# Three unused pads that shift the start addresses of the wide products' operands in SBUF

## The chip, the core and the metric

The kernel runs on one core of a Trainium2 chip. The core has five engines that run beside each other and meet through semaphores: TensorE (PE in the profile, its weight loads shown apart as PEld), VectorE (DVE), ScalarE (ACT), GpSimd (POOL) and SyncE (SP, which here issues nearly all DMAs). Operands lie in SBUF, 128 partitions wide; a tile takes the same byte range in each partition, so its place is one start address. Products go to PSUM.

The metric is the device time of one execution in microseconds, the median of several runs. Before the change it is 1610.83 us over three runs, from 1602.51 to 1612.37.

## The reference

One layer of an encoder block on 1024 tokens of width 1024, in float32:

```python
h = rms_norm(h_res, norm_w[layer])
z = jnp.einsum('bsd,dc->bsc', h, w_in[layer])
qkv_a, g_a, q_b, zf_fwd, zf_bwd, i_b, g_b, zgate_a, zgate_b = jnp.split(z, split_points, axis=-1)
...
y_a = jnp.einsum('bsc,cd->bsd', o_a * jax.nn.silu(g_a), w_proj_a[layer])
...
y_b = jnp.einsum('bsc,cd->bsd', o_b, w_proj_b[layer])
merged = jax.nn.sigmoid(zgate_a) * y_a + jax.nn.sigmoid(zgate_b) * y_b
h_res = h_res + jnp.einsum('bsd,de->bse', merged, w_out[layer])
```

Three groups of windowed attention (dilations 1, 4 and 16) give o_a; a gated linear recurrence in both directions gives o_b. Most of the arithmetic is the four dense products: the input projection (1024 by 12288), the two branch projections and the output projection.

## The kernel before

**Wide products.** Each dense product is cut into matmuls with a stationary operand of 128x128 and a moving operand of 128x512. To keep float32 accuracy every operand is split into a rounded part and the rest (float32r tiles: whi and wlo for the weights, hhi and hlo for the normalised input, sh and sl or mh and ml for later inputs), and three matmuls are run for each block: high with high, high with low, low with high. There are 5496 such matmuls. ScalarE rounds, GpSimd or VectorE subtracts, and a page of 128x512 weights is then used by 24 matmuls.

Which operand moves depends on the stage. In `tok_group` (line 773) the weights move and slices of hhi and hlo, 128 tokens each, are stationary; for the second and third attention group `tok_view` (line 760) takes tokens with a stride of 4 or 8 elements. In `T_group` (line 785) hhi and hlo move and the weights are stationary. `run_quads` (line 425) computes most of the two branches' merging gates by block products with sums of halves (tiles S0 to S3, each with a high and a low part). At the end `three` (line 1704) runs the branch projections, with sh and sl moving, and the last loop runs the output projection, with the weights moving and mh and ml stationary. Only the first four value tiles, at the very start, use uhi and ulo.

**Order.** All instructions pass through one helper (`call`, line 54 and 55, so that the profile shows every instruction at L55), which keeps a plan of each engine's time. A scheduler in Python (`Builder`) fills the gaps between wide products with small ones (scores, transposes, the recurrence) when the plan says that their inputs are ready. The plan is worked out from sizes and types; it does not look at addresses. The result is a fixed order on each engine, with semaphores where one engine needs another.

**Stages**, in us of the profiled execution: opening and first attention group to about 200, second group to about 390, third to about 600, gates and early pages with the merging of the attention groups to 829, block products 829 to 943, recurrence with its projections about 970 to 1370, branch projections to 1513, output projection to the end.

**Where the tiles lie.** SBUF is handed out from two stacks, in the order in which pools and tiles are declared, each tile rounded up to 32 bytes. The left stack begins at 16512, behind a reserved range and four constants:

```python
    consts = ctx.enter_context(tc.tile_pool(name="consts", bufs=1))
    wpool = ctx.enter_context(tc.tile_pool(name="wts", bufs=1))
    stg = ctx.enter_context(tc.tile_pool(name="stg", bufs=3))
    tiny = ctx.enter_context(tc.tile_pool(name="tiny", bufs=2))
```

consts holds nw, hwc, ident and nqk: 32 + 32 + 512 + 32 = 608 bytes. wts (raw, whi, wlo) and stg hold tiles of 2048 bytes. tiny is 2624 bytes long. Behind it come the pools of each stage, one after another at the same place. The right stack begins at 229344 and grows downwards; hhi and hlo, 32768 bytes each, are its first tiles, and the S sums or the tail's sh and sl stand below or in place of them. This gives the start addresses of before, modulo 128 bytes:

| tiles | region | start modulo 128 |
|---|---|---|
| ident | left, consts | 64 |
| raw, whi, wlo, stage | left, wts and stg | 96 |
| hhi, hlo, S0 to S3 | right | 96 |
| sh, sl of the second branch | right | 96 |
| sh, sl of the first branch, mh, ml, uhi, ulo | left, behind tiny | 32 |
| ig, qr, km, sk, kT of the attention, s, pT, zn, v | left, behind tiny | 32 |
| S, xa, on, kT of the recurrence | left, behind tiny | 96 |
| dg (moving operand of rB, `spread`, line 691) | left, behind tiny | 0 |

Of the kernel before, what the change touches and what calls it, by code (L numbers as in the profile page):

```python
# [8 lines left out]
F32 = mybir.dt.float32  # L9
# [555 lines left out]
def hybrid_block(ctx, tc, a, out):  # L565
    b = Builder(ctx, tc, a)
    a_, v_, g_, t_, s_ = b.p.act, b.p.dve, b.p.pool, b.p.pe, b.p.sp
# [4 lines that stand above are left out]
# [2 lines left out]
    bps = ctx.enter_context(tc.tile_pool(name="bps", bufs=5, space=PSUM))  # L574
    b.gps = b.ring(gps, "g", 3, [128, 512])
    b.bank = b.ring(bps, "b", 5, [128, 512])
    hctx = ExitStack()
    hpool = hctx.enter_context(tc.tile_pool(name="hT", bufs=1, side="right"))
    ctx.enter_context(tc.manual_schedule())
# [1294 lines left out]
def _build(arrays):  # L1874
    import concourse.bacc as _bacc
    nc = _bacc.Bacc("TRN2", target_bir_lowering=False, num_devices=1)
    args = {n: nc.dram_tensor(f"in_{n}_dram", v.shape, mybir.dt.from_np(v.dtype), kind="ExternalInput").ap()
            for n, v in arrays.items()}
    out = nc.dram_tensor("out_0_dram", (S, D), F32, kind="ExternalOutput").ap()
    with tile.TileContext(nc) as tc:  # L1880
        hybrid_block(tc, args, out)
    return nc
# [9 lines left out]
```

## Time and profile before

| | before |
|---|---|
| median of three runs | 1610.83 us |
| lowest and highest | 1602.51 and 1612.37 us |
| profiled execution | 1608.46 us |
| its span, first to last instruction | 1606.6 us |
| mean granted TensorE clock | 0.99 |
| LDWEIGHTS and MATMUL instructions | 8373 each |
| moved by DMA | 148 MB in 110,879 packets |

A row of the timeline gives the start in us, the length, the engine, the operation with out<-in (the moving operand is named first, the stationary one second), the shapes and how many alike were merged; in brackets stand idle time before it and what ended that. A row of a group gives busy time and the mean of one in ns, then the idle time before. Starts of matmuls are recorded, their ends are modelled, so the length of one (389 ns) is more than the distance to the next start.

### The profile page before, as it was taken

How to read it: one execution, taken by the hardware profiler on the slowest of the kernel's cores; microseconds unless marked ns; L12 is line 12 of the kernel's file. 1: busy time of each engine (PE TensorE's matmuls, PEld its weight loads, DVE VectorE, ACT ScalarE, POOL GpSimd, SP SyncE). 2: the span in 40 equal slices, each digit the busy share in tenths (PEclk: the TensorE clock that was granted, in tenths of full speed). 3: DMA queues.
4: the chain of work that ended last, by engine and by line, in shares of the span. 5: the costliest groups of instructions: out<-in, count | busy, mean ns of one | idle time of the engine just before them, and what ended most of it. 6: DMA issues, size and time to landing. Idle time of an engine off the chain costs nothing. (4 is left out here: it accounts for less than half of the span.)

```text
span 1606.6 us, 23188 instructions
## 1 busy us (share of the span) xinstructions
PE 1569.1 (98%) x8373; PEld 1335.8 (83%) x8373; DVE 845.3 (53%) x2216; ACT 659.5 (41%) x1434; POOL 468.0 (29%) x462
## 2 busy tenths in 40 slices
PE   8899999999999999999899999999999999999999
PEld 6688899999999987678788888888877878888887
DVE  5667632575136642336412207988889887543211
ACT  5533542434334363213334437655565554422110
POOL 3411202202022031228434434433344423003320
PEclk9999999999999999899999999999999999999999
DMA  6402203102022035473413251121221211842232
GB/s 215 139 22 98 70 18 112 50 33 67 21 63 66 16 103 138 125 219 112 144 66 115 83 166 40 53 93 40 54 86 47 94 39 65 293 140 92 88 119 89
DMA packets 110879, 148.31 MB, mean 92 GB/s; under 512 B 24625, under 2 KB 48300, under 8 KB 110764
## 3 DMA queue, kind: packets, MB, share of 16 engines
q1 hardware_dynamic: 103340, 146.38, 29.1%
q8 instruction: 66, 1.08, 0.3%
q10 hardware_dynamic: 7424, 0.45, 0.3%
q14 instruction: 49, 0.40, 0.1%
HBM read 110.77 MB, written 40.73 MB: 94 GB/s over the span
## 5 line engine op out<-in xcount | busy, mean ns | idle before, releaser
L55 POOL TENSOR_TENSOR wlo<-raw,whi 128x512 fp32r<-128x512 f32 x192 | 253.9, 1328 | 685.8 <-ACT whi L55 670.4
L55 PE MATMUL gp<-whi,hhi 128*128 128x512 f32 x792 | 328.5, 415 | 8.3 <-ACT stage L55 5.7
L55 PE MATMUL gp<-wlo,hhi 128*128 128x512 f32 x792 | 316.0, 399 | 1.4 <-POOL wlo L55 1.4
L55 PE MATMUL gp<-whi,hlo 128*128 128x512 f32 x792 | 316.1, 399 | 0.0
L55 PEld LDWEIGHTS gp<-whi,hhi 128*128 128x128 f32 x792 | 200.5, 253 | 36.8 <-issue 10.0
L55 PEld LDWEIGHTS gp<-wlo,hhi 128*128 128x128 f32 x792 | 201.4, 254 | 18.3 <-POOL wlo L55 2.6
L55 PEld LDWEIGHTS gp<-whi,hlo 128*128 128x128 f32 x792 | 200.9, 254 | 17.9 <-DVE hlo L55 1.0
L55 PE MATMUL gp<-hhi,whi 128*128 128x512 f32 x512 | 209.4, 409 | 0.0
L55 PE MATMUL gp<-hhi,wlo 128*128 128x512 f32 x512 | 200.9, 392 | 0.0
L55 PE MATMUL gp<-hlo,whi 128*128 128x512 f32 x512 | 200.0, 391 | 0.0
L55 ACT ACTIVATE whi<-raw 128x512 fp32r<-128x512 f32 x192 | 119.3, 626 | 140.9 <-PE gp L55 81.7
L55 PEld LDWEIGHTS gp<-hhi,wlo 128*128 128x128 f32 x512 | 96.2, 188 | 21.3
L55 PEld LDWEIGHTS gp<-hhi,whi 128*128 128x128 f32 x512 | 96.8, 189 | 18.8 <-issue 1.0
L55 PEld LDWEIGHTS gp<-hlo,whi 128*128 128x128 f32 x512 | 96.8, 189 | 17.2
L55 ACT ACTIVATE s<-s,neg 128x192 f32<-128x192 f32 (+2 forms) x192 | 83.9, 439 | 65.5 <-DVE neg L55 65.3
L55 DVE TENSOR_REDUCE ss<-sq 128x8 f32<-128x512 f32 x48 | 32.8, 684 | 146.7 <-ACT sq L55 146.7
L55 POOL TENSOR_TENSOR wlo<-qraw,whi 128x512 fp32r<-128x512 f32 x42 | 55.0, 1316 | 76.9 <-ACT whi L55 76.7
L55 PE MATMUL gp<-sh,whi 128*128 128x512 f32 x192 | 75.0, 391 | 0.0
L55 PE MATMUL gp<-sh,wlo 128*128 128x512 f32 x192 | 74.9, 390 | 0.0
L55 PE MATMUL gp<-sl,whi 128*128 128x512 f32 x192 | 74.6, 389 | 0.0
L55 ACT ACTIVATE sq<-gp 128x512 f32<-128x512 f32 x48 | 28.0, 592 | 111.8 <-PE gp L55 91.4
L55 ACT ACTIVATE stage<-gp 128x512 f32<-128x512 f32 x48 | 28.0, 594 | 111.5 <-PE gp L55 88.3
(225 smaller groups left out, 2787.9 us busy)
## 6 DMA issues: line engine op xcount, KB each, us to landing
raw<-in_w_in_dram SPq DMA_DIRECT2D x168, 256.0 KB
igD<-stage SPq DMA_DIRECT2D x32, 256.0 KB
ig<-igD SPq DMA_DIRECT2D x32, 256.0 KB
sgl<-sgD SPq DMA_DIRECT2D x32, 256.0 KB
oD<-os SPq DMA_DIRECT2D x48, 128.0 KB
og<-oD SPq DMA_DIRECT2D x24, 256.0 KB
qraw<-in_w_in_dram SPq DMA_DIRECT2D x24, 256.0 KB
sgD<-spare SPq DMA_DIRECT2D x24, 256.0 KB
```

Source lines behind the costliest of these rows:

```text
L55: got = f(*args, **kw)
```

## The change

Three tiles are declared that no instruction writes or reads.

```diff
     b.gps = b.ring(gps, "g", 3, [128, 512])
     b.bank = b.ring(bps, "b", 5, [128, 512])
+    top = ctx.enter_context(tc.tile_pool(name="top", bufs=1, side="right"))
+    top.tile([128, 24], F32, name="topPad")
+    consts.tile([128, 8], F32, name="lowPad")
+    tiny.tile([128, 16], F32, name="tinyPad", bufs=1)
     hctx = ExitStack()
     hpool = hctx.enter_context(tc.tile_pool(name="hT", bufs=1, side="right"))
```

lowPad takes 32 bytes at the start of consts, so ident, the weights, stage and tiny begin 32 bytes later. tinyPad takes 64 bytes at the start of tiny, so everything behind tiny begins 96 bytes later. topPad takes 96 bytes at the top of the right stack, so everything on that side begins 96 bytes lower. Modulo 128 the wide products' tiles then begin at 0 in all regions, ident at 96, ig, qr, km and sk at 0, S, xa and on at 64, and dg at 96.

## The prediction

> **What bounds the kernel now.** I read the page's busy shares and its 40 slices first, then the timeline of TensorE (matmuls and weight loads), the groups by form, the sums by windows, and last the waits.
>
> ```profile
> span 1606.6 us, 23188 instructions
> PE 1569.1 (98%) x8373; PEld 1335.8 (83%) x8373; DVE 845.3 (53%) x2216; ACT 659.5 (41%) x1434; POOL 468.0 (29%) x462
> PE   8899999999999999999899999999999999999999
> PEclk9999999999999999899999999999999999999999
> ```
>
> TensorE is busy in 98% of the span at a granted clock of nearly 1, so the time is the number of its instructions times the distance from one start to the next. 5496 of its 8373 matmuls are wide products, a moving operand of 128x512 float32r. Busy time can't give that distance (the ends are modelled and overlap); the timeline's starts can. Here is the block-product stage, where every operand of both kinds starts at 96 modulo 128 bytes:
>
> ```profile
> 829.21 0.39 PE L55 MATMUL qA<-hhi,whi 128*128 128x512 f32 x1
> ...
> 834.65 0.39 PE L55 MATMUL qA<-S1h,whi 128*128 128x512 f32 x1
> ```
>
> There are 24 products from the first start to the last: 5.44 / 24 = 226.7 ns each. Under the half clock, early in the kernel, the distance is another (first a stretch of the windows view: length, PE busy, granted clock, DMA; then the timeline):
>
> ```profile
> 30.00:36.00 6.00, 5.44 (x17) 0.50 0.47 171
> ```
> ```profile
> 32.86 0.63 PE L55 MATMUL u<-wlo,uhi 128*128 128x512 f32 x1
> 33.29 0.63 PE L55 MATMUL u<-whi,ulo 128*128 128x512 f32 x1
> 33.71 0.63 PE L55 MATMUL u<-whi,uhi 128*128 128x512 f32 x1
> ```
>
> 0.85 / 2 = 425 ns for 512 columns, 0.83 ns a column. At the full clock 512 columns would need half of that, 213 ns, and take 226.7. So some 13 ns are not columns through the array: they are hidden when the array runs slowly and show when it runs fast. That is what a feed of the moving operand that can't quite keep up looks like. Is it the next weight load, read at the same time?
>
> ```profile
> 767.68 0.39 PE L55 MATMUL gp<-whi,hlo 128*128 128x512 f32 x1
> 773.75 0.80 PE L55 MATMUL gp<-whi,hhi 128*128 128x512 f32 x1 [5.68 <-ACT stage L55]
> ```
> ```profile
> 767.46 0.19 PEld L55 LDWEIGHTS gp<-whi,hlo 128*128 128x128 f32 x1
> 773.75 0.29 PEld L55 LDWEIGHTS gp<-whi,hhi 128*128 128x128 f32 x1 [6.10 <-ACT stage L55]
> ```
>
> No weight load runs beside the product at 767.68, the next comes 6 us later, and it still lasts 0.39 us like those in the chain. So the 13 ns belong to the moving stream itself. 226.7 / 213.3 is 17 / 16, and 2048 bytes that begin 32 bytes short of a 128-byte boundary touch 17 such pieces instead of 16. That arithmetic carries the forecast; it is an inference, no row here shows an aligned wide product.
>
> Do start addresses matter at all? Two stages of before have other starts. With the stationary operand (mh, ml) at 32 and the moving one at 96, and then with the moving operand (sh, sl) at 32 and the stationary one at 96:
>
> ```profile
> 1520.09 0.40 PE L55 MATMUL gp<-whi,mh 128*128 128x512 f32 x1
> ...
> 1523.59 0.39 PE L55 MATMUL gp<-whi,mh 128*128 128x512 f32 x1
> ```
> ```profile
> 1390.29 0.39 PE L55 MATMUL gp<-sh,whi 128*128 128x512 f32 x1
> ...
> 1392.35 0.39 PE L55 MATMUL gp<-sh,whi 128*128 128x512 f32 x1
> ```
>
> 3.50 / 15 = 233.3 ns and 2.06 / 9 = 228.9 ns, against 226.7, for the same shapes and types. So the starts do count, by 2 to 7 ns.
>
> Two attention groups have stationary operands with a stride (4 or 8 elements between columns):
>
> ```profile
> 219.64 0.39 PE L55 MATMUL gp<-whi,hhi 128*128 128x512 f32 x1
> ...
> 222.22 0.40 PE L55 MATMUL gp<-whi,hlo 128*128 128x512 f32 x1
> ```
> ```profile
> 408.94 0.41 PE L55 MATMUL gp<-whi,hhi 128*128 128x512 f32 x1
> ...
> 411.63 0.41 PE L55 MATMUL gp<-whi,hlo 128*128 128x512 f32 x1
> ```
> ```profile
> L55 PEld LDWEIGHTS qA<-hlo,whi 128*128 128x128 f32 x47 | 8.8, 188 | 1.8
> L55 PEld LDWEIGHTS gp<-whi,hhi 128*128 128x128 f32 x157 | 48.7, 310 | 1.9 <-issue 1.9
> L55 PEld LDWEIGHTS gp<-whi,hhi 128*128 128x128 f32 x176 | 57.9, 329 | 2.2 <-issue 1.4
> ```
>
> 2.58 / 11 = 234.5 ns (stride 4) and 2.69 / 11 = 244.5 ns (stride 8). Their loads last 310 and 329 ns against 188, longer than the distance: there the weights are likely the limit, not the stream.
>
> **The change part by part.** It adds three tiles that nobody writes or reads: no instruction, DMA, wait or semaphore. The order on every engine is worked out from sizes and not from addresses, so it stays. What moves are start addresses: everything in the left stack behind lowPad by 32 bytes, behind tinyPad by 96, everything in the right stack by 96 downwards. whi, wlo, hhi, hlo, the S sums, uhi, ulo, mh, ml, sh and sl all come to 0 modulo 128 (the strided views start 4r bytes further).
>
> The target distance. The only wide moving operand at 0 modulo 128 in this trace is dg, in two passes at two cycles a column:
>
> ```profile
> 53.31 1.02 PE L55 MATMUL rB<-dg,ones 128*128 128x512 f32 x2
> L55 PE MATMUL rB<-dg,ones x4: 591/592/593, 38.5 to 53.7; 128*128 128x512 f32 x4
> ```
>
> (The second row is from the view of the tile rB.) Start to start is 1.02 - 0.59 = 0.43 us for 1024 cycles, 427 by the array: an excess of some 2 to 3 ns. It streams at half the rate, so it doesn't prove the point, but it is the nearest row. I take 215.7 ns; the bounds are 213.3 (all excess gone) and 233.3 (0 modulo 128 as bad as the mh pairing).
>
> [...]
>
> The terms, products counted from the loops:
> - Both at 96, contiguous: 3648 products, 11.0 ns each: 40.1 us.
> - Moving 96, stationary 32: 504, of which 96 lie in the opening 48 us, whose pace loads and preparation set (taken as nothing); 408 x 17.6 = 7.2 us.
> - Moving 32, stationary 96: 192 x 13.2 = 2.5 us.
> - Strided: 2 x 576. Bounds 0 (weights limit) and 11 ns (stream limits); the loads' row is nearer, so I take 3 ns: 3.5 us, bounds 0 and 12.7.
> - Other operands move too. ident goes from 64 to 96; if a stream of 512 bytes pays a quarter of 13.4 ns, 691 transposes cost 2.3 us; those that read ig, S, qr and pT (now at 0 or 64) could win as much. Taken as nothing, bounds -2.3 and 2.3. DVE, ACT and POOL work on the same shapes; none of them bounds.
>
> Sum: 53.3 us off TensorE's own time. What of it reaches the end?
>
> ```profile
> 48.00:200.00 152.00, 149.12 (x850) 119.09 (x849) 99.10 (x358) 67.81 (x184) 34.05 (x31) 1.00 0.27 84
> 970.00:1100.00 130.00, 126.78 (x780) 106.17 (x779) 112.93 (x234) 79.44 (x148) 55.21 (x69) 0.99 0.19 58
> 1200.00:1300.00 100.00, 96.12 (x641) 81.74 (x641) 86.62 (x192) 55.19 (x101) 37.33 (x47) 1.00 0.20 64
> PE gp L55 <- ACT stage L55: 5.7, 1, 5.7
> PE U L55 <- ACT kT L55: 5.5, 4, 2.6
> PE oB L55 <- DVE S L55: 5.4, 4, 3.2
> ```
>
> (Columns of the first three: stretch, then busy time of PE, PEld, DVE, ACT, POOL. The last three are waits: total, times, longest.) In the recurrence stage, 970 to 1370, DVE is 87% busy and TensorE already waits for it. A DVE chain behind each head doesn't shorten, so I let a third of that stage's gain (1174 products, 12.9 us) be lost: 4.3. The stage wait that ends at 773.75 stands behind some 690 products since 600 us, which gain 7.6 us; if the stores that free the buffers don't come sooner, the wait grows by that; I take 3. The early attention, where DVE is two thirds busy, 1 us. Lost: 8.3. Bounds of the loss: nothing, and 12.9 + 7.6 if others set both stretches.
>
> 53.3 - 8.3 = 45.0 us. The profiled execution took 1608.46 us (1606.6 of span and 1.9 around it): 1563.5. It lies 2.4 below the median of the runs shown, 1610.83. Forecast: 1563.
>
> **The rivals.**
> (a) The 13 ns don't come from the start. They could be the price of four-byte operands at the full clock, wherever they begin; no row excludes it, since all wide streams of before start at 32 or 96. For it: the starts 96 and 32 both pay about the same 13 ns. Against it: the exact 17 / 16, and that pairings of starts move the distance. Then only the mixed pairings go to 226.7: 408 x 6.6 + 192 x 2.2 = 3.1 us, 1605. [...]
> (b) Slower. A weight load starts one distance ahead of its product (767.46 and 767.68 above), so beside the whole stream before it; with both at 0 modulo 128 the two streams could collide as at 96 with 32. Price: 6.6 ns on each of 3648 products, 24 us, and 192 x 4.4 = 0.8; no gain elsewhere: 1633. Against it: 96 with 96, the same phase, has the lowest distance of all. It decides against me from a distance above 226.7 in the block stage; above 231 (16 / 3648 is 4.4 ns more) it is slower by over 1%.
> (c) The stream gets shorter but is eaten: the strided products gain nothing, and the recurrence and the stretch ahead of the stage wait keep their length, set by DVE, ACT and the stores. For it: the waits shown. Against it: TensorE is 96 to 98% busy there and the others 87% at most. Left: 53.3 - 3.5 - 12.9 - 7.6 = 29.3 us, 1579.
> (d) The pads don't land where meant. The lengths (608 + 32 bytes of consts, 2624 + 64 bytes of tiny, 96 at the top) come to multiples of 128, so I give it nothing.
>
> **How the numbers follow.** The forecast's case gets 0.48, (c) 0.17, (a) 0.27, (b) 0.08. The time is the first's. Its own range is 1536 (213.3 on the 4248 contiguous products: 10.2 us more; strided by 11 ns: 9.2; no losses: 8.3; together 1535.8) to 1575. The range must take in (c) and (a) with its bound of 2.3 for ident: 1536 to 1607. What a measurement of this kernel can tell from no change is about 1%, 16 us. Faster by over 1%: 0.48 + 0.17 = 0.65. Within 1%: (a), 0.27. Slower: (b), 0.08.
>
> **What would show it.** In the changed kernel the block stage decides: 24 products there in 5.18 us is right, 5.44 is rival (a), more than that (b). The mh stage should fall to the same distance as the block stage. Strided distances near 234 and 244 with loads of 310 and 329 ns say that weights bind there; a fall by 11 says that the stream did. Waits of U and oB for DVE and the stage wait should be longer by some 8 us in all. The same instruction count and the same order must be found. The forecast is wrong if the distance at 0 modulo 128 stays at 226.7.

## The result, and the profile after

| | before | after |
|---|---|---|
| median | 1610.40 us | 1622.84 us |
| lowest and highest of six runs | 1602.51 and 1612.37 us | 1621.90 and 1624.14 us |
| span of the profiled execution | 1606.6 us | 1620.3 us |
| mean granted TensorE clock | 0.990 | 0.993 |

The changed kernel takes 1.0084 times as long as the one before (95% interval 1.0063 to 1.0105): about 13 us slower, where 45 us faster were forecast. Instructions (23188) and DMA traffic (110879 packets, 148.31 MB) are the same. From the page of the changed kernel, the span and the busy times:

```profile
span 1620.3 us, 23188 instructions
PE 1586.2 (98%) x8373; PEld 1339.9 (83%) x8373; DVE 845.4 (52%) x2216; ACT 659.7 (41%) x1434; POOL 467.8 (29%) x462
```

Against before, PE has 17 us more and VectorE, ScalarE and GpSimd are within 0.3 us. So the time was added by TensorE's own instructions. The block-product stage was named as the place that decides; its timeline in the changed kernel (start, length, operation), the same two products as were shown of before:

```profile
833.56 0.39 PE L55 MATMUL qA<-hhi,whi 128*128 128x512 f32 x1
...
839.14 0.39 PE L55 MATMUL qA<-S1h,whi 128*128 128x512 f32 x1
```

24 products in 5.58 us: 232.5 ns each, where before had 5.44 and 5.18 was hoped for. Taken from all starts, the distance isn't constant now: it repeats over seven products, 232, 231, 232, 228, 230, 233 and 241 ns, 232.4 in the mean. The same mean stands at every wide chain of the changed kernel, the output projection (whi with mh) included, which before had 233.3:

```profile
1532.00 0.40 PE L55 MATMUL gp<-whi,mh 128*128 128x512 f32 x1
...
1535.48 0.39 PE L55 MATMUL gp<-whi,mh 128*128 128x512 f32 x1
```

3.48 / 15 = 232.0 ns. All stages came to one distance, as the prediction expected of equal starts, but to a worse one. The whole difference, from the distances between all starts of matmuls in the two traces, in us (a chain is a run of wide products that follow each other without a wait or another kind of product between them):

| distances | before | after |
|---|---|---|
| wide, contiguous, inside chains | 4039 of 228.41 ns: 922.6 | 4046 of 232.39 ns: 940.3 |
| the same, 262 ns and longer (waits, half clock, a group's first) | 73.7 | 69.2 |
| the same, to another kind of product | 41.9 | 41.0 |
| strided by 4, inside chains | 536 of 235.1 ns: 126.0 | 536 of 239.2 ns: 128.2 |
| strided by 8, inside chains | 534 of 244.9 ns: 130.8 | 534 of 245.6 ns: 131.2 |
| all else | 306.4 | 305.4 |

The products inside chains cost 17.7 + 2.6 us more (1.6 of it because seven more of them fall into the first row), and 6 to 7 us of that come back in the other rows, which leaves the 13.7 by which the span grew. By stage, with the same product marking the ends in both kernels:

| stage of before, us | wide contiguous products | after minus before, us |
|---|---|---|
| to 48 | 122 | -0.2 |
| 48 to 200 | 454 | +1.3 |
| 200 to 600 (mostly strided) | 96 | +2.7 |
| 600 to 829 | 864 | +0.5 |
| 829 to 970 | 622 | +3.6 |
| 970 to 1370 | 1174 | +3.1 |
| 1370 to 1513 | 628 | +3.1 |
| 1513 to the end | 383 | -0.4 |

Between 829 and 970, where TensorE waits for nothing (no distance above 227 ns before and 241 ns after), the 622 products pay 5.7 ns each, the full step from 226.7 to 232.4. From 600 to 829 almost all of it is given back. The windows of that stretch, before and then after (stretch, length, busy time of PE, PEld, DVE, ACT, POOL, granted clock, DMA share, GB/s), and TensorE's waits after (total, times, longest):

```profile
600.00:829.00 229.00, 219.18 (x957) 174.06 (x954) 88.11 (x112) 64.10 (x119) 82.81 (x59) 0.96 0.45 135
```
```profile
600.00:829.00 229.00, 221.35 (x958) 173.13 (x957) 86.50 (x112) 66.60 (x129) 80.06 (x57) 0.97 0.44 135
```
```profile
PE oB L55 <- DVE S L55: 5.3, 4, 3.2
PE U L55 <- ACT kT L55: 4.6, 3, 2.1
PE gp L55 <- ACT stage L55: 4.5, 1, 4.5
```

TensorE comes to the stage wait 4.3 us later than before (at 772.37 us, before at 768.07), and the wait ends 3.1 us later (776.84, before 773.75): it fell from 5.7 to 4.5 us, and over the whole stretch the distances of 262 ns and more, of products with 512 columns, fell from 36.5 to 31.9 us. Part of that is pace: 17 wide distances of the stretch are at half pace (400 to 450 ns), where before had 23, and the granted clock is a little higher (0.97, before 0.96). That isn't simply because the waits are shorter: behind the shorter stage wait there are 8 of them, where before had 6. The other two rows are waits of the recurrence, which had 5.4 (oB) and 5.5 us (U) before.

### The profile page after: what moved, and what is told of

It reads as the page before. It is cut to its first block, busy times and chain, and to the rows that moved or that the text cites. A ratio compares the mean times of both kernels' runs of the same rounds, so it can differ in the third digit from the quotient of the medians.

```text
span 1620.3 us, 23188 instructions
## 1 busy us (share of the span) xinstructions
PE 1586.2 (98%) x8373; PEld 1339.9 (83%) x8373; DVE 845.4 (52%) x2216; ACT 659.7 (41%) x1434; POOL 467.8 (29%) x462
## 2 busy tenths in 40 slices
DMA packets 110879, 148.31 MB, mean 92 GB/s; under 512 B 24625, under 2 KB 48300, under 8 KB 110764
```

## The experiments

The block stage had become slower at 0 with 0 modulo 128, as rival (b) has it. Whether that is the reason was asked of wide products with nothing else beside them first; the theory that came out of the first table (what counts is how far the start of the weights lies from that of the moving operand, modulo 256) was then tested against (b) and against the forecast's own reason. Four kernels measure wide products alone, five move the tiles of the kernel itself.

**t1_table: all pairings of starts.** The kernel is replaced: only chains of 84 wide products that add up in one PSUM tile, nothing beside them, and the output is the last sum. The moving tile starts at 0, 32, 64 or 96 modulo 128 (A to D), the stationary one likewise.

```diff
+    for m in "ABCD":
+        for w in "ABCD":
+            last = chain("p" + m + w, mov[m], sta[w])
```

> This kernel computes nothing of the reference: it runs 16 chains of 84 wide float32r products (128x512 moving, 128x128 stationary) with nothing beside them, one chain for each pair of start addresses 0, 32, 64, 96 modulo 128 of the moving and the stationary operand, and stores one of the results. Theory 1, the pairing of the two starts sets the distance of wide products by itself: the four pairs known from the two traces come out as there (moving 96 with stationary 96: 226.7 ns; 96 with 32: 233.3; 32 with 96: 228.9; 0 with 0: 232.4), and the other twelve fill the table, some perhaps below 226.7. Theory 2, the extra distance in the changed kernel comes from other traffic whose tiles moved too: all sixteen are alike, within 1 ns. My forecast's 17/16 rule would give 213 to 216 for every pair whose moving operand starts at 0; the 0 with 0 stage of the changed kernel has already contradicted it.

The timeline, some of the chains (start, length of the whole chain, name, and how many products):

```profile
26.39 19.68 PE L39 MATMUL pAA<-mA,wA 128*128 128x512 f32 x84
45.91 19.75 PE L39 MATMUL pAB<-mA,wB 128*128 128x512 f32 x84
65.50 19.39 PE L39 MATMUL pAC<-mA,wC 128*128 128x512 f32 x84
84.72 19.76 PE L39 MATMUL pAD<-mA,wD 128*128 128x512 f32 x84
...
299.94 19.83 PE L39 MATMUL pDC<-mD,wC 128*128 128x512 f32 x84
319.60 19.68 PE L39 MATMUL pDD<-mD,wD 128*128 128x512 f32 x84
```

From start to start a chain AA takes 19.52 us, 232.4 ns a product; AC 19.22, 228.8; DC 19.66, 234.0. Means over the last 42 distances of each chain, in ns:

| moving \ stationary | A | B | C | D |
|---|---|---|---|---|
| A | 232.4 | 233.3 | 228.9 | 233.3 |
| B | 234.3 | 232.4 | 233.3 | 228.9 |
| C | 233.3 | 234.3 | 232.4 | 233.3 |
| D | 233.3 | 233.3 | 234.3 | 232.4 |

All four diagonal fields are equal: 0 with 0 is no worse and no better than 96 with 96. And 96 with 96 gives 232.4 here, though before's block stage, 96 with 96 as well, ran at 226.7. So the start modulo 128 doesn't settle the distance, neither as the forecast had it nor as (b) had it. Modulo 256 the two cases differ: here the moving tiles start at 128, 160, 192 and 224, the stationary ones at 0, 32, 64 and 96, so that on the diagonal stationary minus moving is 128. In before hhi and whi both start at 224 modulo 256, difference 0; in the changed kernel at 128 and 0. Fields of the table with the same difference modulo 256 have nearly the same value: 192 gives 228.9 twice, 96 gives 234.3 three times, 128 gives 232.4 four times. Before's own mixed stages fit in: sh with whi is difference 192 and had 228.9, whi with mh is 64 and had 233.3.

**t2_width: element size and length.** Again chains alone, with bfloat16 operands, and with float32r at 512 columns and fewer.

```diff
+    for m, w in ("AA", "BB", "DD", "DB", "DA", "AD"):
+        chain("b" + m + w, bm[m], bw[w])
+    for n in (512, 448, 384, 256, 128):
+        for m, w in ("AA", "DD", "DB"):
+            chain("n..." + m + w, mov[m], sta[w], n)
```

> This kernel computes nothing of the reference either: chains of 63 products, first bfloat16 operands at 512 columns for six pairs of starts (0/0, 32/32, 96/96, 96/32, 96/0, 0/96), then float32r at 512, 448, 384, 256 and 128 columns for the pairs 0/0, 96/96 and 96/32. If the excess over columns / 2.4 GHz belongs to reading four bytes a column, bfloat16 shows some 216 ns for every pair, and with float32r the excess (13 to 20 ns at 512) shrinks in proportion with the columns (3 to 5 ns at 128). If it is a fixed cost for each product or for each weight load, bfloat16 or the narrow products keep 13 ns or more.

The timeline (four chains of 63), then two groups of weight loads (busy time, mean of one in ns):

```profile
35.45 13.76 PE L47 MATMUL bBB<-bmB,bwB 128*128 128x512 bf16 x63
49.04 13.76 PE L47 MATMUL bDD<-bmD,bwD 128*128 128x512 bf16 x63
...
118.07 14.86 PE L47 MATMUL nhDD<-mD,wD 128*128 128x512 f32 x63
132.76 14.87 PE L47 MATMUL nhDB<-mD,wB 128*128 128x512 f32 x63
```
```profile
L47 PEld LDWEIGHTS <-bwB 128*128 128x128 bf16 x126 | 12.3, 98 | 14.9
L47 PEld LDWEIGHTS nhAA<-mA,wA 128*128 128x128 f32 x63 | 11.9, 188 | 2.8
```

bfloat16: 13.59 / 63 = 215.7 ns, and 215.8 for all six pairings. float32r at the same 512 columns: 14.69 / 63 = 233.2. So the aligned distance that the forecast took for float32r exists, but for bfloat16, and there it needs no alignment. A bfloat16 load lasts 98 ns, a float32r load 188. With fewer float32r columns the two differences 128 and 64 give 203.8 and 202.2 ns (448), 175.9 and 174.7 (384), 118.7 and 113.3 (256), and 111.7 for both at 128. The columns' own time is an estimate from the half clock of before (granted clock 0.50 from 30 to 36 us), where the timeline has

```profile
32.86 0.63 PE L55 MATMUL u<-wlo,uhi 128*128 128x512 f32 x1
...
35.42 0.63 PE L55 MATMUL u<-wlo,uhi 128*128 128x512 f32 x1
```

Six products take 2.56 us, 426.7 ns each; half of that is 213.3 ns for 512 columns, and fewer in proportion. The excess over it is 15 to 20 ns from 384 columns up and 7 to 12 at 256. It neither goes with the length nor is it constant. DD at 512 columns had 233.3 here and 232.4 in t1_table with the same addresses, with another repeating pattern: a chain can settle into more than one.

**t3_diff: the difference in steps of 16 bytes.** One moving tile, and a wide tile of weights from which the stationary start is moved by 16 bytes from chain to chain (ra to rp); then fewer weight columns, and strides.

```diff
+    for k in range(16):
+        chain("r" + letters[k], m, W[:, 4 * k:4 * k + 512])
```

> This kernel computes nothing of the reference: chains of 57 float32r products with the stationary start moved against a fixed moving start in 16 steps of 16 bytes (differences 0 to 240 modulo 256), some of them again after other chains, then chains with only 64 or 32 stationary columns, with a stationary stride of 4 and 8, and single products that each wait for ScalarE, float32r and bfloat16. Theory D, the moving stream and the next weight load hinder each other, and what counts is the difference of their starts modulo 256: 226.7 ns at difference 0, 232.4 at 128, 228.9 at 192, 233.3 at 64 as in the first table; fewer stationary columns bring the distance down toward 216; a single float32r product, with no load beside its stream, is as long as a bfloat16 one (379 ns). Rival I, float32r operands cost 11 ns at the full clock in any case and only the rest is pairing: fewer columns stay at 226 or more, and a single float32r product keeps some 389 ns against 379.

The timeline, chains of 57 (ra, rb, rc, rd: differences 0, 16, 32, 48; ri: 128; halfa, halfi: 64 weight columns, differences 0 and 128):

```profile
24.32 13.08 PE L47 MATMUL ra<-mA,W 128*128 128x512 f32 x57
37.24 13.09 PE L47 MATMUL rb<-mA,W 128*128 128x512 f32 x57
50.17 13.45 PE L47 MATMUL rc<-mA,W 128*128 128x512 f32 x57
63.47 13.45 PE L47 MATMUL rd<-mA,W 128*128 128x512 f32 x57
...
129.93 13.47 PE L47 MATMUL ri<-mA,W 128*128 128x512 f32 x57
143.23 13.46 PE L47 MATMUL rj<-mA,W 128*128 128x512 f32 x57
...
314.32 13.27 PE L62 MATMUL halfa<-mA,W 128*64 128x512 f32 x57
327.42 13.34 PE L62 MATMUL halfi<-mA,W 128*64 128x512 f32 x57
```

ra: 12.92 / 57 = 226.7 ns. rb: 12.93, 226.8. rc: 13.30, 233.3. ri: 13.30, 233.3 (232.4 in two repeats). Of the other differences 176 gives 230.1, 240 gives 228.3, 192 gives 233.3 and in two repeats 228.9, and the rest 232.1 to 234.3. So the moving tile at 128 modulo 256 has the fast distance as soon as the weights start there too. Nothing goes below 226.7. Shorter loads don't free the rest: at difference 0, 64 weight columns (loads of 134 ns) have 13.10 / 57 = 229.8, and 32 columns (109 ns) have 231.7 over their last 42 distances, both more than the 226.7 of full loads of 188 ns. Of the expectation's two signs, that of rival I came (226 or more), and theory D's fall toward 216 did not. Strided weights have 235.0 (stride 4) and 244.4 ns (stride 8) alone as in the kernel. Single float32r products that each wait 0.72 us for ScalarE lasted 0.40 to 0.49 us in the first four and 0.80 us from the sixth on, bfloat16 ones 0.58 us after a first of 0.65. With such a spread they can't be held against the 389 and 379 ns of the expectation.

**t4_next: what a product takes over from the one before, and finer steps.** Groups of one float32r product and three of bfloat16; chains whose weights alternate between differences 0 and 128 one by one (swap) or in pairs (pairs); differences of 8, 4, 12 and 252 bytes (fine, finer, finest, back).

```diff
+    for name, offs in (("swap", (0, 32)), ("pairs", (0, 0, 32, 32)), ("fine", (2,)), ("finer", (1,)), ("finest", (3,)), ("back", (63,))):
+        for q in range(REP):
+            s = offs[q % len(offs)] + 128 * (q % 4)
+            nc.tensor.matmul(p, W[:, s:s + 128], m, start=(q == 0), stop=(q == REP - 1))
```

> This kernel computes nothing of the reference. First, one float32r product (difference 0, then 128) followed by three bfloat16 products, over and over: the load beside the float32r stream is a bfloat16 one. If the 13 ns at difference 0 and the 19 at 128 come from the float32r load beside the stream, the distance from a float32r product to the next start falls to about 216 ns in both; if the stream pays its 13 ns alone, it stays at 226.7 in both and only the 6 above it go; if neither is so, 232 stays at difference 128. Then chains whose stationary start alternates between differences 0 and 128 (each load against the same moving operand): a mean near 229 to 233 ns if each product pays for its own pair. Then differences of 4, 8, 12 and 252 bytes: 226.7 if what counts is a 16-byte piece or coarser, as the 0 and 16 of the 16-byte table were alike.

The timeline, chains of 57:

```profile
114.94 13.31 PE L64 MATMUL fine<-mA,W 128*128 128x512 f32 x57
128.09 13.41 PE L64 MATMUL finer<-mA,W 128*128 128x512 f32 x57
141.34 13.28 PE L64 MATMUL finest<-mA,W 128*128 128x512 f32 x57
154.46 13.46 PE L64 MATMUL back<-mA,W 128*128 128x512 f32 x57
167.75 13.09 PE L46 MATMUL end<-mA,W 128*128 128x512 f32 x57
```

fine 230.7, finer 232.5, finest 230.2, back 233.2 ns, by the starts; by their last 42 distances swap has 232.2, pairs 232.9, end (difference 0) 226.7. A difference of 16 bytes was as good as none (226.8 in t3_diff), one of 4, 8 or 12 wasn't. Alternating doesn't give the mean of both distances (229.5 to 230) but the slow one. It lies in the 229 to 233 that were expected, but it speaks against each product paying for its own pair alone: what stands before or behind it in the chain has a part. The mixed groups are inconclusive: a group of four takes 0.90 us with difference 0 and with 128; three bfloat16 distances and one of 226.7 would be 0.87, so the groups take 0.03 us more than that, which is more than the 6 ns that were looked for.

**e_top128: before with 128 bytes at the top of the right stack.** No start of a wide operand changes modulo 128, but hhi, hlo and the S sums now differ from the weights by 128 modulo 256.

```diff
+    top = ctx.enter_context(tc.tile_pool(name="top", bufs=1, side="right"))
+    top.tile([128, 32], F32, name="topPad")
```

> Before with one pad of 128 bytes at the top of the right stack: every start modulo 128 is as before, but hhi, hlo, the S sums and the second branch's sh and sl now differ by 128 modulo 256 from the weights, 3648 products. Theory D: the block stage at 232.4 ns and a time near the change's, 1620 to 1624. The rival that starts modulo 128 decide: no difference to before, 1610.

```profile
835.01 0.39 PE L55 MATMUL qA<-hhi,whi 128*128 128x512 f32 x1
...
840.58 0.39 PE L55 MATMUL qA<-S1h,whi 128*128 128x512 f32 x1
```

Block stage (timeline): 5.57 / 24 = 232.1 ns, with the pattern of seven. Time 1624.21 us, 1.0089 of before (1.0069 to 1.0110). This alone makes a loss as large as the change's, with every alignment modulo 128 kept as it was. (b) falls here, and so does the forecast's reason.

**e_all256: the change with larger pads**, so that every wide operand starts at 0 modulo 256 and all differences are 0.

```diff
+    top.tile([128, 56], F32, name="topPad")
+    consts.tile([128, 8], F32, name="lowPad")
+    tiny.tile([128, 48], F32, name="tinyPad", bufs=1)
```

> The change with larger pads (topPad 224 bytes, lowPad 32, tinyPad 192): every wide operand starts at 0 modulo 256, so at 0 modulo 128 as in the change, and all differences are 0. Theory D: the block stage has 226.7 ns again, the products with mh, ml, sh, sl have it too, and the time is 3 us below before: 1607, ratio 0.998. The rival that a start at 0 modulo 128 is itself bad: as the change, 1622.

Timeline of the block stage and of the output projection:

```profile
829.40 0.39 PE L55 MATMUL qA<-hhi,whi 128*128 128x512 f32 x1
...
834.84 0.39 PE L55 MATMUL qA<-S1h,whi 128*128 128x512 f32 x1
```
```profile
1515.29 0.39 PE L55 MATMUL gp<-whi,mh 128*128 128x512 f32 x1
...
1518.69 0.39 PE L55 MATMUL gp<-whi,mh 128*128 128x512 f32 x1
```

5.44 / 24 = 226.7 and 3.40 / 15 = 226.7 ns. Here, too, all wide operands begin at multiples of 128, as in the changed kernel; the distance is that of before, and the stages that lay at 233.3 and 228.9 come down to it. Time 1606.19 us, 0.9974 of before (0.9963 to 0.9984): 4 us faster, the lowest median of all. In the output projection it ends 2.2 us sooner over 330 products, 6.7 ns each.

**e_tiny192: before with 192 bytes at the start of tiny only.** All wide operands at 224 modulo 256, differences 0, none aligned to 128.

```diff
+    tiny.tile([128, 48], F32, name="tinyPad", bufs=1)
```

> Before with one pad of 192 bytes in tiny: nothing is aligned to 128, the main tiles stay at 96, and uhi, ulo, mh, ml, sh, sl come to 96 too, so that all differences are 0 modulo 256. Theory D: the same as with all starts at 0 modulo 256, 3 us below before. If alignment to 128 or 256 were worth something by itself, this one would be slower than that one.

Block stage:

```profile
829.52 0.39 PE L55 MATMUL qA<-hhi,whi 128*128 128x512 f32 x1
...
834.96 0.39 PE L55 MATMUL qA<-S1h,whi 128*128 128x512 f32 x1
```

5.44 / 24 = 226.7 ns. Time 1608.04 us, 0.9986 of before (0.9974 to 0.9997); mean distance of the contiguous products inside chains 227.49 ns against 227.48 in e_all256. Whether the common start is a multiple of 128 makes no difference to the distance. The 2 us between the two lie, in the profiled executions, inside the recurrence, between 1300 and 1370 above all; why was not pursued.

**e_top96 and e_left: the two halves of the change.** The first has topPad alone (difference 96 in the block stage), the second lowPad and tinyPad alone (difference 32).

```diff
+    top.tile([128, 24], F32, name="topPad")
```

> The change's topPad alone: hhi, hlo, the S sums and the second branch's sh and sl start at 0 modulo 128, the weights stay at 96. Differences modulo 256 (stationary less moving): 96 for 2424 contiguous products, 160 for 1224, 192 and 64 for the rest as before. Theory D by its table (234.3 at 96, 233.3 at 160, against 232.4 at 128 in the change): a little slower than the change, 1623 to 1627, though half of its operands are aligned. The rival that alignment to 128 hurts where it is present: between before and the change, about 1616.

```diff
+    consts.tile([128, 8], F32, name="lowPad")
+    tiny.tile([128, 16], F32, name="tinyPad", bufs=1)
```

> The change's lowPad and tinyPad alone: the weights and all tiles behind tiny start at 0 modulo 128, hhi and hlo stay at 96. Differences: 32 for 2424 contiguous products, 224 for 1224, 128 for 696. Theory D by its table (233.3, 233.3, 232.4): again near the change or a little slower, 1622 to 1626. The rival that each aligned operand adds its share: about 1616.

Block stage of e_top96, then of e_left:

```profile
835.20 0.39 PE L55 MATMUL qA<-hhi,whi 128*128 128x512 f32 x1
...
840.82 0.40 PE L55 MATMUL qA<-S1h,whi 128*128 128x512 f32 x1
```
```profile
833.04 0.40 PE L55 MATMUL qA<-hhi,whi 128*128 128x512 f32 x1
...
838.64 0.40 PE L55 MATMUL qA<-S1h,whi 128*128 128x512 f32 x1
```

5.62 / 24 = 234.2 and 5.60 / 24 = 233.3 ns, the table's values for 96 and 32. Times: 1624.73 us (1.0089, 1.0073 to 1.0106) and 1624.53 (1.0092, 1.0077 to 1.0107). Each half takes the stationary and the moving tiles away from a common start; together they bring them to the other bad place, half of 256 apart. The two losses don't add up.

## Why the prediction was wrong

- **What bounds the kernel** was right: the time is the number of TensorE's products times their distance. A step of 4 ns in the mean distance of the contiguous wide products moved the end by 0.8%.
- **The step that failed** is the inference that the 13 ns come from a start 32 bytes short of a 128-byte boundary, 17 / 16. The ratio was a coincidence: e_tiny192 has 226.7 ns at 96 modulo 128, e_all256 the same 226.7 at 0, and none of the six pairings costs bfloat16 anything. In its place stands the difference between the starts of weights and moving operand modulo 256. In before it was 0 for 3648 products, by the way the stacks happened to be filled; the pads made it 128 for all 4344.
- **The two mixed stages** (233.3 and 228.9 ns) were rightly read as proof that starts count, and wrongly as the price of a misaligned start. They were the differences 64 and 192. Two rows with different starts can't tell a start from a difference of starts; a third, with both starts moved alike, would have.
- **"Is it the next load?"** was answered by a row of a product with no load beside it that lasts 0.39 us like those in the chain. In the changed kernel the same product, again with none beside it, stands in the timeline with the length of its slower chain:

```profile
771.97 0.40 PE L55 MATMUL gp<-whi,hlo 128*128 128x512 f32 x1
776.84 0.50 PE L55 MATMUL gp<-whi,hhi 128*128 128x512 f32 x1 [4.47 <-ACT stage L55]
```

  Its neighbours ahead have 0.39 and 0.40. So the last product, with no load beside it, is as long as its chain whether that is fast or slow (ends are modelled, besides), and an equal length couldn't acquit the weights: their address decides by up to 7.6 ns (t3_diff, with one and the same moving tile).
- **The target distance** of 215.7 ns, taken from the row of rB, is found for bfloat16 and in no float32r chain of these runs. The nearest row was too far: dg's product is two instructions, and at 0.43 us from start to start they run at half the pace of the wide ones (226.7 ns).
- **The terms.** Both at 96: -11.0 ns forecast; +5.7 where the chains run undisturbed. Moving 96 with stationary 32: -17.6 forecast, -0.9 measured (233.3 to 232.4). Moving 32 with stationary 96: -13.2 forecast, +3.5 measured. Strided: -3 forecast, +4.1 and +0.7 measured.
- **Lost at waits.** 8.3 us of a gain were to be eaten by waits; of the loss, 6 to 7 us came back, 4.6 of them in the long distances of 600 to 829, where the stage wait stands. (Ahead of that wait are 627 wide products since 600 us, by the windows view of before, and not some 690; that is 0.7 us of the 7.6.) The recurrence, where VectorE was expected to set the pace, gave next to nothing back: its wide distances below 262 ns rose by 3.3 ns (229.2 to 232.5), the long ones stayed (42.4 us both times), and the waits of U and oB fell by 1.0 us in all.
- **Rival (b)** had the sign, nearly the price (6.6 ns, measured 5.7 in the block stage) and the thought that load and stream meet, which no run here shows directly. Its condition was wrong, since 0 with 0 modulo 128 is fast when it is 0 with 0 modulo 256. The argument against it, that equal phase had the lowest distance, was sound; what was missed is that the pads don't keep the phase equal modulo 256. (a) was right that float32r pays whatever its start (no chain below 226.7, bfloat16 215.8), but not in expecting that nothing gets worse. (c) had nothing to act on, since the stream didn't get shorter.
- **Left open**: why float32r at difference 0 still takes 11 ns more than bfloat16. The number of weight columns isn't the reason (t3_diff); moving bytes and element size weren't told apart. That the difference of starts decides is shown; why it does is not. Open, too, is what makes the repeating patterns, and whether the weights that count are the product's own or the next one's; all weights of a chain had the same start modulo 256, or alternated.

## What to carry to other kernels

Where a float32r kernel is bound by back-to-back wide matmuls, look at the start addresses of both operands, and try stationary and moving tiles at the same start modulo 256 bytes: here that had 226.7 ns, against 232 to 234 at most other differences. A common start at a multiple of 128 was worth nothing by itself (227.48 ns at 0 modulo 256 in e_all256, 227.49 at 224 in e_tiny192). An added or resized tile can break such an accident of layout: 96 bytes at one end of SBUF cost this kernel some 14 us (e_top96, 1.0089 of before). When an edit is to move one quantity, list which others move with it (here the difference of two starts), and look for rows that hold one still.

## What the hardware showed that was not expected

- Wide float32r products had distances between 226.7 and 234.3 ns in the chains of t1_table and t3_diff, by stationary minus moving start modulo 256: 226.7 at 0 and 16, 228.3 at 240, 228.9 at 192 in most chains, 230.1 at 176, 232 to 234 elsewhere on the 16-byte grid. That 256 is the period is borne out by whole kernels, where differences modulo 1024 of 0, 256, 512 and 768 have means of 227.0 to 227.7 ns (e_all256), and 128, 384, 640 and 896 of 232.2 to 232.6 (the changed kernel).
- bfloat16 products of the same 128x512 didn't show it: 215.8 ns for six pairings in t2_width (differences 32, 64, 128 and 224).
- Most slow pairings didn't have a steady distance but cycles of two to seven products; the widest cycle, in the changed kernel's block stage, ran from 228 to 241 ns. The chains of t4_next that alternate between difference 0 and 128 ran at the slow one's pace (232.2 and 232.9 ns).
